# Gate and up products of an FFN by sevenfold block products: high and low part of the input joined in one matmul, low parts of stored weights by adding DMAs

## The chip, the cores and the metric

The kernel runs on one core of a Trainium2 chip. Its metric is device microseconds of one execution. A core has five engines that run side by side, each through its own list of instructions in order: TensorE (PE, with its weight loads shown apart as PEld), VectorE (DVE), ScalarE (ACT), GpSimd (POOL) and SyncE (SP). PSUM, where TensorE writes its sums, has eight banks of 512 fp32 values per partition; SBUF holds all else that is on the chip.

## The reference, cut to what matters

One layer of a decoder over 512 tokens of width 1024, all in fp32:

```python
x = x + 0.5 * RMSNorm_post(SwiGLU_1(RMSNorm_pre(x)))    # FFN 1
h = RMSNorm_pre(x)
y = mixer(h)                    # dilated attention, mLSTM, gates, output projection
x = x + RMSNorm_post(y)
x = x + 0.5 * RMSNorm_post(SwiGLU_2(RMSNorm_pre(x)))    # FFN 2

def swiglu(x, w_gate, w_up, w_down):    # 1024x2816, 1024x2816, 2816x1024
    return (silu(x @ w_gate) * (x @ w_up)) @ w_down
```

Only the gate and up products of the two FFNs, silu(x @ w_gate) * (x @ w_up), are the subject here.

## The kernel before, in words

Every large matmul is made of three: each fp32 value v is cast to a shorter type (fp32r) as its high part h, and v - h is its low part l. A product of weights and input is then h h + h l + l h, summed in PSUM. Casts run on ScalarE, the subtractions on VectorE. In the names below wh and wl are the parts of a weight, hTh and hTl those of the normalised input, which lies transposed (1024 on partitions in 8 chunks, 512 tokens along the free axis; `new_hT`, line 211, two tiles).

The hidden width 2816 is cut into 22 blocks f of 128. In each FFN f = 0 and 1 go through `by_halves` and f = 2 through `ws`, both plain. The 19 blocks f = 3 to 21 go through `seven` (lines 299 to 419), a scheme in the manner of Strassen and Winograd. It takes the two weight blocks of one f, gate g and up u, each cut into two halves of the 1024 sums (g0, g1, u0, u1, 128x512 each with four chunks of 128 side by side), and the input cut into 2x2 blocks, halves of the sums by halves of the tokens (256 tokens each). Instead of eight block products it makes seven, numbered 1 to 7, whose factors are sums of blocks:

- weights: 1 = g0, 2 = g1, 4 = u1 as stored; 7 = ab0 = g0 + u0 and 5 = ab1 = u0 + u1; 6 = cd0 = ab0 + u1 and 3 = cd1 = cd0 + g1. Signs are in the stored weights.
- input: made once per FFN by `token_parts` (line 269): parts 1, 2, 3 are blocks of hTh and hTl, parts 4 to 7 are sums, split anew in tiles of their own.

One `product` (line 336) is 12 matmuls of 256 columns: for each of the four chunks, wh times the input's high part and wh times its low part, and then wl times the high part for each chunk. A unit (one f) has thus 84 matmuls. Its results stand in two PSUM banks, one column half each: bank qa holds a (products 1 and 2: gate, first tokens; the copy q1 takes product 1 alone), bank qb holds b (6, then 7, then 4) and c (5, then 3) in its two halves. VectorE and ScalarE combine them:

- q1 = copy of a behind product 1 (ScalarE)
- uv = (b, c) + q1 behind products 6 and 5, one operation over the whole bank qb
- `inner`, behind products 7 and 3: z1 = b + uv1 and z2 = c + uv0, two operations of 256 columns
- `finish`, behind product 4, which goes on into b: z0 = b + q1, then aT = -(z0, z1) * s in one operation (aT is the FFN's hidden activation)
- silu(0): s0 = silu(a) behind product 2; silu(1): s1 = silu(z2)

The weights' path per unit: `load` issues two DMAs of 512 KB (g and u) on SP into tiles wf (three buffers, line 311). `take` casts a pair of blocks to wh on ScalarE and returns the subtraction that makes wl on VectorE; it is used for (1, 2) from g (`front`), (4) from u1, (6, 3) from cd and (7, 5) from ab. `sums` are four additions on VectorE. Tiles wh and wl have five buffers, those of (4) two; scr tiles: ab, cd, uv and s one buffer each, q1 and z two.

The order of each engine is written out by hand. `do` is an object of class `Order` (line 259): it issues each instruction behind the last one of the same engine, so VectorE, ScalarE, POOL and SP run exactly in program order, and all of these instructions carry line 265 in the trace. TensorE runs in program order too (line 340). The loop (lines 376 to 417) goes over units u, with v the next unit and w the one after. TensorE's order for one u is product 1 of u, 6, 5, product 4 of the previous unit, then 2, 7, 3 of u. Between them stand, in program order: `inner` and silu(1) of the previous unit; q1; the low part of (1, 2) of v; the loads of w; `sums` of v and the cast of cd; uv; the low part of cd; z0 and aT of the previous unit; the cast and low part of (4) of v; silu(0) of u; the cast and low part of ab of v; the cast of g of w.

A PSUM tile comes from `bank` (line 62), a pool of eight banks in rotation (line 60), which all stages of the kernel share. Behind `seven` follows the down projection, its first part also sevenfold (class `Down`, 35 steps). It is a generator: its first pieces (loads, sums, splits and `banks` for eight accumulators, lines 583 to 585) run between the last units of `seven` by `next(ahead)`. Its weights are summed by adding DMAs on POOL's queue (`add`, accum_op=ADD), its T and S tiles take the buffers of hTh and hTl (lines 587 and 588). `ffn` (line 607) puts the stages together, lines 638 to 650.

Of the kernel before, what the change touches and what calls it, by code (L numbers as in the profile page):

```python
# [10 lines left out]
F32 = mybir.dt.float32  # L11
# [28 lines left out]
def tile_hybrid_block(ctx: ExitStack, tc: tile.TileContext, a: dict):  # L40
# [153 lines left out]
    def by_halves(groups, hTh, hTl, todo):  # L194
        for hf in range(2):
            tok = slice(hf * T // 2, (hf + 1) * T // 2)
            for n, (outs, ws_) in enumerate(groups):
# [4 lines left out]
                for i, b in order:  # L202
# [5 lines left out]
                    if hf == 0 and b and (n, i) in FLUSH:  # L208
                        flush(todo)

    def new_hT(name):
        hTh = hpool.tile([P, KD, T], F32R, tag="hTh", name=f"hTh_{name}")
        hTl = hpool.tile([P, KD, T], F32R, tag="hTl", name=f"hTl_{name}")
        return hTh, hTl

# [53 lines left out]
    def token_parts(low, tmp, hTh, hTl, name):  # L269
        def quad(t, i, j):  # L270
            return t[:, 4 * i:4 * i + 4, j * H:(j + 1) * H]

        hf, xs_ = tmp[:, 0:8, :], tmp[:, 8:16, :]
        for j in (1, 0):
            for i in (1, 0):
                with tc.issue_after(opened[0]):
                    nc.vector.tensor_tensor(quad(hf, i, j), quad(hTh, i, j).bitcast(F32),
                                            quad(hTl, i, j).bitcast(F32), op=ADD)
        b11, b12, b21, b22 = (quad(hf, i, j) for i in range(2) for j in range(2))
        f = {k: xs_[:, 2 * i:2 * i + 2, :].rearrange("p a (b c) -> p (a b) c", c=H) for i, k in enumerate((5, 6, 7, 4))}  # L280
        parts = {1: (quad(hTh, 0, 0), quad(hTl, 0, 0)), 2: (quad(hTh, 1, 0), quad(hTl, 1, 0)),
                 3: (quad(hTh, 1, 1), quad(hTl, 1, 1))}

        def part(k):
            xh, xl = (low.tile([P, 4, H], F32R, name=f"x{k}{x}_{name}") for x in "hl")
            split(f[k], xh, xl)
            parts[k] = (xh, xl)
# [11 lines left out]
    def seven(do, fs, wgu, x, low, scr, aT, name, ahead):  # L299
        tt = lambda out, p, q, op: do("vector", "tensor_tensor", out, p, q, op=op)  # L300
        cast = lambda out, p: do("scalar", "copy", out, p)

        class Unit:
# [3 lines left out]
            def load(self):  # L307
                self.gu = []
                for b in range(2):
                    t = act.tile([P, 2, Q], F32, tag="wf", bufs=3, name=f"{'gu'[b]}_{self.n}")  # L310
                    nc.sync.dma_start(t, wgu[self.f, :, b * 1024:(b + 1) * 1024].rearrange("p (q c) -> p q c", c=Q))
                    self.gu.append(t)

            def take(self, keys, src, n=2):
                pool, tag, bufs = (wpool, "", 5) if n == 2 else (low, "4", 2)
# [20 lines left out]
            def product(self, out, k, first, last):  # L336
                (wh, wl), (xh, xl) = self.w[k], x[k]
                terms = [(wh, y, i) for i in range(4) for y in (xh, xl)] + [(wl, xh, i) for i in range(4)]
                for n, (wt, y, i) in enumerate(terms):
                    nc.tensor.matmul(out, lhsT=wt[:, i * P:(i + 1) * P], rhs=y[:, i, :], start=first and n == 0,  # L340
                                     stop=last and n == len(terms) - 1, skip_group_check=True)

            def open(self):
                n = self.n
                self.pa, self.pb = bank(f"qa_{n}"), bank(f"qb_{n}")
                self.q1 = scr.tile([P, H], F32, tag="q1", bufs=2, name=f"q1_{n}")
                self.uv = scr.tile([P, 2, H], F32, tag="uv", bufs=1, name=f"uv_{n}")
                self.z = scr.tile([P, 3, H], F32, tag="z", bufs=2, name=f"z_{n}")
                self.s = scr.tile([P, 2, H], F32, tag="s", bufs=1, name=f"s_{n}")
                self.a, self.b, self.c = self.pa[:, 0:H], self.pb[:, 0:H], self.pb[:, H:T]  # L350
# [15 lines left out]
        for u in us[:2]:  # L366
            u.load()
            u.front()
            if u is us[0]:
                u.low12()  # L370
                u.sums()
                u.lowcd()
                u.take((4,), u.gu[1][:, 1:2, :], 1)()
                u.take((7, 5), u.ab)()
        prev = None
        for i in range(len(fs)):
# [21 lines left out]
            if v:  # L398
# [32 lines left out]
    class Down:  # L431
# [138 lines left out]
        def run(self):  # L570
# [11 lines left out]
            self.split(s1, "x")  # L582
            ba, bd, bc, bb = (self.banks(*x) for x in (("a", (0, 1), 0), ("d", (2, 3), 1), ("c", (0, 1), 1),
                                                       ("b", (2, 3), 0)))
            self.out = {"1": bd, "2": ba, "3": bc, "4": bb, "5": bc, "6": bb, "7": bb}
            self.product(s0)
            self.T = hpool.tile([P, KD, T], F32, tag="hTh", name=f"T_{self.name}")
            self.S = hpool.tile([P, KD, T], F32, tag="hTl", name=f"S_{self.name}")
            for g in range(4):
                self.do("sync", "dma_start", self.U(g), self.B(g, BLOCK["1"]))  # L590
            yield
            self.T4 = self.xp.tile([P, self.n4, T], F32, tag="u4", bufs=1, name=f"T4_{self.name}")
            self.S4 = self.xp.tile([P, self.n4, H], F32, tag="s4", bufs=1, name=f"S4_{self.name}")
# [13 lines left out]
    def ffn(pool, todo, first_w, hT, wgu, wdq, wdh, wd, post, finish, name, begin=None, pins=(), aT=None):  # L607
# [1181 lines left out]
```

## Time and profile before

| | us |
|---|---|
| runs, three: lowest, median, highest | 1311.48, 1312.67, 1314.56 |
| profiled execution, its own time | 1310.56 |
| its span, first to last instruction | 1308.6 |
| TensorE busy | 1300.7 (99%) |
| TensorE weight loads busy | 1179.0 (90%) |
| VectorE busy | 1039.5 (79%) |
| ScalarE busy | 658.2 (50%) |
| GpSimd busy | 124.9 (10%) |
| granted TensorE clock, mean | 0.999 |
| moved by DMA | 182.72 MB, mean 140 GB/s |

The profile is that of one execution. Busy times are sums of instruction durations, and matmuls overlap, so the durations of single matmuls (0.28 us for one of 256 columns) are longer than the distance from one start to the next. In a table by line, a row gives the line, the engine, the operation, the output and inputs with their shape, the count, the busy time and the mean of one in ns, then the idle time of the engine ahead of them and what ended it. In a row of the timeline the first number is the start in us, the second the duration; a bracket gives a wait of the engine ahead of the instruction and its releaser. The names of tiles carry _a in FFN 1 and _b in FFN 2. A DMA's row gives its queue (SPq, POOLq), its size and the time from issue to landing.

### The profile page before, as it was taken

How to read it: one execution, taken by the hardware profiler on the slowest of the kernel's cores; microseconds unless marked ns; L12 is line 12 of the kernel's file. 1: busy time of each engine (PE TensorE's matmuls, PEld its weight loads, DVE VectorE, ACT ScalarE, POOL GpSimd, SP SyncE). 2: the span in 40 equal slices, each digit the busy share in tenths (PEclk: the TensorE clock that was granted, in tenths of full speed). 3: DMA queues.
4: the chain of work that ended last, by engine and by line, in shares of the span. 5: the costliest groups of instructions: out<-in, count | busy, mean ns of one | idle time of the engine just before them, and what ended most of it. 6: DMA issues, size and time to landing. Idle time of an engine off the chain costs nothing.

```text
span 1308.6 us, 20788 instructions
## 1 busy us (share of the span) xinstructions
PE 1300.7 (99%) x8173; PEld 1179.0 (90%) x8173; DVE 1039.5 (79%) x1599; ACT 658.2 (50%) x1065; POOL 124.9 (10%) x175
## 2 busy tenths in 40 slices
PE   9999999999999999999999999999999999999997
PEld 9999999888899888888888889998889999999886
DVE  7999988888895577577798687666389998897887
ACT  6444444566644546435555554434265444445563
POOL 1000000231302110011112010000010000001220
PEclk9999999999999999999999999999999999999999
DMA  5233333696458974257637532334412333325981
GB/s 195 96 113 97 112 101 111 180 245 152 152 170 223 320 91 134 68 158 183 210 90 178 169 97 65 102 108 161 168 61 81 111 101 110 112 99 155 268 174 65
DMA packets 52114, 182.72 MB, mean 140 GB/s; under 512 B 6133, under 2 KB 7181, under 8 KB 51761
## 3 DMA queue, kind: packets, MB, share of 16 engines
q1 hardware_dynamic: 32832, 116.18, 27.0%
q0 software_dynamic: 19168, 65.22, 20.9%
q8 instruction: 64, 1.05, 0.3%
q14 instruction: 34, 0.27, 0.1%
q10 hardware_dynamic: 16, 0.00, 0.0%
HBM read 171.87 MB, written 9.46 MB: 139 GB/s over the span
## 4 chain that ended last, share of the span: by engine, by line
PE 99%; DVE 1%; POOL 0%; issue 0%; ACT 0%; DVEq 0%; POOLq 0%; ACTq 0%
PE qb_a L340 10%; PE qb_b L340 10%; PE pq L191 8%; PE pm L191 7%; PE qa_b L340 4%; PE qa_a L340 4%; PE qb_gm L1209 4%; PE acc_o L245 3%; PE accb_b L539 3%; PE vo1p L940 3%; PE vo0p L940 3%; PE w12p L940 3%; PE accb_a L539 3%; PE accc_b L539 2%; PE accc_a L539 2%; PE pg_a L205 2%
## 5 line engine op out<-in xcount | busy, mean ns | idle before, releaser
L191 PE MATMUL pq<-hTh_mx,wh_qk 128*128 128x512 f32 x160 | 63.2, 395 | 0.0
L191 PE MATMUL pq<-hTl_mx,wh_qk 128*128 128x512 f32 x160 | 62.4, 390 | 0.0
L191 PE MATMUL pm<-hTh_mx,wh_mqk 128*128 128x512 f32 x128 | 50.4, 394 | 0.0
L191 PE MATMUL pm<-hTl_mx,wh_mqk 128*128 128x512 f32 x128 | 49.9, 390 | 0.0
L101 DVE TENSOR_TENSOR wl_qk<-wf_qk,wh_qk 128x1024 fp32r<-128x1024 f32 x24 | 29.3, 1221 | 17.6 <-ACT wh_qk L85 13.5
L265 ACT CAST wh_a<-cd_a 128x1024 fp32r<-128x1024 f32 x19 | 19.9, 1049 | 40.8 <-DVE cd_a L265 40.8
L265 ACT CAST wh_b<-cd_b 128x1024 fp32r<-128x1024 f32 x19 | 19.9, 1049 | 40.5 <-DVE cd_b L265 40.5
L191 PE MATMUL pq<-hTh_mx,wl_qk 128*128 128x512 f32 x160 | 39.5, 389 | 0.0
L85 ACT CAST wh_qk<-wf_qk 128x1024 fp32r<-128x1024 f32 x24 | 25.0, 1045 | 28.6 <-PE pq L191 12.1
L340 PE MATMUL qa_b<-hTh_f,wh_b 128*128 128x256 f32 x152 | 38.2, 284 | 0.0
L340 PE MATMUL qa_a<-hTh_f,wh_a 128*128 128x256 f32 x152 | 38.2, 284 | 0.0
L340 PE MATMUL qa_b<-hTl_f,wh_b 128*128 128x256 f32 x152 | 38.1, 283 | 0.0
L340 PE MATMUL qa_a<-hTl_f,wh_a 128*128 128x256 f32 x152 | 38.1, 283 | 0.0
L1117 DVE SCALAR_TENSOR_TENSOR z<-pm,cw,z 128x511 f32<-128x511 f32 (+2 forms) x48 | 35.3, 743 | 2.2 <-ACT z L1115 1.8
L191 PEld LDWEIGHTS pq<-hTh_mx,wl_qk 128*128 128x128 f32 x160 | 30.0, 188 | 6.2
L191 PEld LDWEIGHTS pq<-hTh_mx,wh_qk 128*128 128x128 f32 x160 | 30.1, 188 | 6.0
L191 PEld LDWEIGHTS pq<-hTl_mx,wh_qk 128*128 128x128 f32 x160 | 30.1, 188 | 6.0
L265 DVE TENSOR_TENSOR wl_b<-ab_b,wh_b 128x1024 fp32r<-128x1024 f32 x19 | 23.3, 1225 | 15.0 <-ACT wh_b L265 15.0
L265 DVE TENSOR_TENSOR wl_a<-ab_a,wh_a 128x1024 fp32r<-128x1024 f32 x19 | 23.3, 1225 | 14.7 <-ACT wh_a L265 14.7
L265 POOL DMA_DIRECT2D T_a<-in_wdq x12 | 10.9, 1155 | 238.3 <-DVE xl_a L265 228.9
L265 POOL DMA_DIRECT2D T_b<-in_wdq x12 | 10.6, 1127 | 236.6 <-PE acca_b L539 225.7
L101 DVE TENSOR_TENSOR wl_mqk<-wf_mqk,wh_mqk 128x1024 fp32r<-128x1024 f32 x16 | 19.5, 1220 | 16.2 <-PE pq L191 8.4
(1021 smaller groups left out, 4654.6 us busy)
## 6 DMA issues: line engine op xcount, KB each, us to landing
wf_qk<-in_wqk SPq DMA_DIRECT2D x24, 512.0 KB, 4.2
g_a<-in_wgu SPq DMA_DIRECT2D x19, 512.0 KB, 3.7
u_a<-in_wgu SPq DMA_DIRECT2D x19, 512.0 KB, 3.7
g_b<-in_wgu SPq DMA_DIRECT2D x19, 512.0 KB, 3.7
u_b<-in_wgu SPq DMA_DIRECT2D x19, 512.0 KB, 3.7
wf_mqk<-in_wmqk SPq DMA_DIRECT2D x16, 512.0 KB, 3.6
wf_vo<-in_wvo SPq DMA_DIRECT2D x16, 512.0 KB, 3.7
T_a<-in_wdq POOLq DMA_DIRECT2D x12, 512.0 KB, 10.3
```

The lines of the kernel that those rows point to most:

```text
L85: return nc.scalar.copy(wh, wf)
L101: last_low[0] = nc.vector.tensor_tensor(wl[:, :m], wf[:, :m], wh[:, :m].bitcast(F32), op=ALU.subtract).ins
L191: nc.tensor.matmul(out, lhsT=wt[:, k * P:(k + 1) * P], rhs=x[:, k, 0:T], start=n == 0, stop=n == len(terms) - 1)
L205: nc.tensor.matmul(outs[b][:, tok], lhsT=ws_[b][w][:, k * P:(k + 1) * P], rhs=x[:, k, tok], start=i + k + hf == 0, stop=hf == 1 and i == 2 ...
L245: nc.tensor.matmul(out, lhsT=x[:, tk], rhs=w[:, cs], start=first and n == 0, stop=last and n == 2, skip_group_check=True)
L265: self.last[eng] = getattr(getattr(nc, eng), fn)(*args, **kw).ins
L340: nc.tensor.matmul(out, lhsT=wt[:, i * P:(i + 1) * P], rhs=y[:, i, :], start=first and n == 0, stop=last and n == len(terms) - 1, skip_gro ...
L539: nc.tensor.matmul(o, lhsT=x[:, tk], rhs=w[:, cs], start=k in "1256" and g + m + n == 0, stop=False, skip_group_check=True)
L940: nc.tensor.matmul(out[k][i], lhsT=x[:, 2 * g + m, i * P:(i + 1) * P], rhs=y[:, m * T:(m + 1) * T], start=k in "156" and g + m + j == 0, s ...
L1117: nc.vector.scalar_tensor_tensor(z[:, s:], src[:, :T - s], cw[:, ct, 3 - s:4 - s], z[:, s:], op0=ALU.mult, op1=ALU.add)
L1209: nc.tensor.matmul(out, lhsT=wt[:, i * P:(i + 1) * P], rhs=y[:, i, :], start=first and m == 0, stop=last and m == len(terms) - 1, skip_gro ...
```

## The change

It has these parts, all in `seven` and what surrounds it.

- The input's high and low parts lie in one tile. `new_hT` allocates one tile [128, 2, 8, 512], and hTh and hTl are its two halves; parts 4 to 7 get one tile [128, 2, 4, 256] each. For products 3 to 7 the matmul with wh then takes 512 columns in one instruction, 256 of the high part and 256 of the low part; the result fills a whole bank, wh times high in its first half (`high`) and wh times low in its second (`low`). The matmul with wl goes into the first half. A product is then 4 matmuls of 512 columns and 4 of 256. Products 1 and 2 keep their 12 of 256 in a half bank.
- b and c need a whole bank each, a pair `qbc`, two such pairs in rotation, and a has a bank `qa`, two in rotation: six banks, in a pool `pairs` that is open during `seven` alone. For this the pool of eight becomes one of two (`psum2`), open throughout, and one of six that is closed ahead of `seven` and opened again behind it (`Banks`); `bank` goes through the six and then the two. `Down` takes the two banks of `psum2` ahead of the others, which it takes when the pairs are closed.
- The halves are added on VectorE: `outer` (high + q1, then low + that) in place of uv's one operation, over (b, c), 512 columns each; `inner` two operations of 512 in place of two of 256; z0 two of 256 in place of one.
- The low parts of the weights that are used as stored, (1, 2) and (4), are no longer subtracted on VectorE. ScalarE writes -wh into wl (`mul` by -1, behind the cast), and an adding DMA on POOL's queue adds the stored weights to it from HBM (`stored`), 512 KB for (1, 2) and 256 KB for (4). These two VectorE operations of 1024 and 512 columns go.
- `Down`'s T and S become one tile, in the buffer of the joined hT.

The diff, cut to its core:

```diff
     def bank(name):
-        return psum.tile([P, 512], F32, tag="pp", name=name)
+        pool = banks.pool if banks.n % 8 < 6 else psum2
+        banks.n += 1
+        return pool.tile([P, 512], F32, tag="pp", name=name)
...
     def new_hT(name):
-        hTh = hpool.tile([P, KD, T], F32R, tag="hTh", name=f"hTh_{name}")
-        hTl = hpool.tile([P, KD, T], F32R, tag="hTl", name=f"hTl_{name}")
-        return hTh, hTl
+        whole_of.append(hpool.tile([P, 2, KD, T], F32R, tag="hT", name=f"hT_{name}"))
+        return whole_of[-1][:, 0], whole_of[-1][:, 1]
...
-            def take(self, keys, src, n=2):
+            def take(self, keys, src, n=2, stored=None):
...
                 cast(wh, src)
-                return lambda: tt(wl, src, wh.bitcast(F32), SUB)
+                if stored is None:
+                    return lambda: tt(wl, src, wh.bitcast(F32), SUB)
+                do("scalar", "mul", wl, wh.bitcast(F32), -1.0)
+                do("gpsimd", "dma_start", wl, stored, accum_op=ADD)
...
             def front(self):
-                self.low12 = self.take((1, 2), self.gu[0])
+                self.take((1, 2), self.gu[0], 2, self.stored(0))
...
             def product(self, out, k, first, last):
-                (wh, wl), (xh, xl) = self.w[k], x[k]
-                terms = [(wh, y, i) for i in range(4) for y in (xh, xl)] + [(wl, xh, i) for i in range(4)]
-                for n, (wt, y, i) in enumerate(terms):
-                    nc.tensor.matmul(out, lhsT=wt[:, i * P:(i + 1) * P], rhs=y[:, i, :], start=first and n == 0,
-                                     stop=last and n == len(terms) - 1, skip_group_check=True)
+                (wh, wl), y = self.w[k], x[k]
+                cols = lambda i: slice(i * P, (i + 1) * P)
+                if k > 2:
+                    terms = [(out, wh[:, cols(i)], y[:, :, i, :]) for i in range(4)]
+                else:
+                    terms = [(out, wh[:, cols(i)], y[:, j, i, :]) for i in range(4) for j in range(2)]
+                terms += [(out[:, 0:H], wl[:, cols(i)], y[:, 0, i, :]) for i in range(4)]
+                for n, (o, w, v) in enumerate(terms):
+                    nc.tensor.matmul(o, lhsT=w, rhs=v, start=first and n == 0, stop=last and n == len(terms) - 1,
+                                     skip_group_check=True)
...
             def open(self):
                 n = self.n
-                self.pa, self.pb = bank(f"qa_{n}"), bank(f"qb_{n}")
+                self.a = pairs.tile([P, 512], F32, tag="qa", bufs=2, name=f"qa_{n}")[:, 0:H]
+                self.bc = pairs.tile([P, 2, 512], F32, tag="qbc", bufs=2, name=f"qbc_{n}")
+                self.b, self.c = self.bc[:, 0], self.bc[:, 1]
+                self.high, self.low = self.bc[:, :, 0:H], self.bc[:, :, H:T]
...
+            def outer(self):
+                z = self.z[:, 1:3, :]
+                tt(z, self.high, self.q1[:, None, :].broadcast_to([P, 2, H]), ADD)
+                tt(self.uv[:, ::-1, :], self.low, z, ADD)
 
             def inner(self):
-                tt(self.z[:, 1, :], self.b, self.uv[:, 1, :], ADD)
-                tt(self.z[:, 2, :], self.c, self.uv[:, 0, :], ADD)
+                z = self.z[:, 1:3, :]
+                tt(z, self.high, self.uv, ADD)
+                tt(z, self.low, z, ADD)
...
             def finish(self):
                 self.product(self.b, 4, False, False)
-                tt(self.z[:, 0, :], self.b, self.q1, ADD)
+                z = self.z[:, 0, :]
+                tt(z, self.b[:, 0:H], self.q1, ADD)
+                tt(z, self.b[:, H:T], z, ADD)
...
-            if v:
-                v.low12()
             u.product(u.b, 6, True, False)
...
-            u.product(u.c, 5, False, False)
-            tt(u.uv, u.pb.rearrange("p (a b) -> p a b", b=H), u.q1[:, None, :].broadcast_to([P, 2, H]), ADD)
+            u.product(u.c, 5, True, False)
+            u.outer()
...
             if v:
-                low4 = v.take((4,), v.gu[1][:, 1:2, :], 1)
-                low4()
+                v.take((4,), v.gu[1][:, 1:2, :], 1, v.stored(1)[:, 1:2, :])
...
         ahead = d.run()
-        last = seven(do, range(PLAIN, NF), wgu, x, low, scr, aT, name, ahead)
+        banks.ctx.close()
+        banks.n = 6
+        pctx = ExitStack()
+        pairs = pctx.enter_context(tc.tile_pool(name=f"pairs_{name}", bufs=2, space=bass.MemoryType.PSUM,
+                                                reuse_waits="tile"))
+        last = seven(do, range(PLAIN, NF), wgu, x, low, scr, pairs, aT, name, ahead)
         dn = ExitStack()
         next(ahead)
         last()
+        pctx.close()
+        banks.open(f"psum6_{name}")
```

More of the change, by code (lines that the diff above doesn't have):

```diff
@@ L59, in tile_hybrid_block, with open @@
     small = ctx.enter_context(tc.tile_pool(name="small", bufs=4, side="right"))
-    psum = ctx.enter_context(tc.tile_pool(name="psum", bufs=8, space=bass.MemoryType.PSUM))
+    psum2 = ctx.enter_context(tc.tile_pool(name="psum2", bufs=2, space=bass.MemoryType.PSUM))
+    class Banks:
+        ctx, pool, n = None, None, 0
+        def open(self, name, n=0):
+            self.ctx, self.n = ExitStack(), n
+            self.pool = self.ctx.enter_context(tc.tile_pool(name=name, bufs=6, space=bass.MemoryType.PSUM))
+    banks = Banks()
+    banks.open("psum6")
+    ctx.callback(lambda: banks.ctx.close())
     def bank(name):
-        return psum.tile([P, 512], F32, tag="pp", name=name)
+        pool = banks.pool if banks.n % 8 < 6 else psum2
+        banks.n += 1
+        return pool.tile([P, 512], F32, tag="pp", name=name)
     def pair(name):
@@ L209, in by_halves @@
                         flush(todo)
+    whole_of = []
     def new_hT(name):
-        hTh = hpool.tile([P, KD, T], F32R, tag="hTh", name=f"hTh_{name}")
-        hTl = hpool.tile([P, KD, T], F32R, tag="hTl", name=f"hTl_{name}")
-        return hTh, hTl
+        whole_of.append(hpool.tile([P, 2, KD, T], F32R, tag="hT", name=f"hT_{name}"))
+        return whole_of[-1][:, 0], whole_of[-1][:, 1]
     def down(n, chunk_src, get_x, post, finish, todo, name, accs=None, first=0):
@@ L280, in token_parts @@
         f = {k: xs_[:, 2 * i:2 * i + 2, :].rearrange("p a (b c) -> p (a b) c", c=H) for i, k in enumerate((5, 6, 7, 4))}
-        parts = {1: (quad(hTh, 0, 0), quad(hTl, 0, 0)), 2: (quad(hTh, 1, 0), quad(hTl, 1, 0)),
-                 3: (quad(hTh, 1, 1), quad(hTl, 1, 1))}
+        parts = {k: whole_of[-1][:, :, 4 * i:4 * i + 4, j * H:(j + 1) * H]
+                 for k, (i, j) in {1: (0, 0), 2: (1, 0), 3: (1, 1)}.items()}
         def part(k):
-            xh, xl = (low.tile([P, 4, H], F32R, name=f"x{k}{x}_{name}") for x in "hl")
-            split(f[k], xh, xl)
-            parts[k] = (xh, xl)
+            x = low.tile([P, 2, 4, H], F32R, name=f"x{k}_{name}")
+            split(f[k], x[:, 0], x[:, 1])
+            parts[k] = x
         nc.vector.tensor_tensor(f[5], b11, b12, op=SUB)
@@ L297, in token_parts, with seven @@
         return parts
-    def seven(do, fs, wgu, x, low, scr, aT, name, ahead):
+    def seven(do, fs, wgu, x, low, scr, pairs, aT, name, ahead):
         tt = lambda out, p, q, op: do("vector", "tensor_tensor", out, p, q, op=op)
@@ L310, in load, with stored @@
                     t = act.tile([P, 2, Q], F32, tag="wf", bufs=3, name=f"{'gu'[b]}_{self.n}")
-                    nc.sync.dma_start(t, wgu[self.f, :, b * 1024:(b + 1) * 1024].rearrange("p (q c) -> p q c", c=Q))
+                    nc.sync.dma_start(t, self.stored(b))
                     self.gu.append(t)
-            def take(self, keys, src, n=2):
+            def stored(self, b):
+                return wgu[self.f, :, b * 1024:(b + 1) * 1024].rearrange("p (q c) -> p q c", c=Q)
+            def take(self, keys, src, n=2, stored=None):
                 pool, tag, bufs = (wpool, "", 5) if n == 2 else (low, "4", 2)
@@ L369, in seven @@
             if u is us[0]:
-                u.low12()
                 u.sums()
                 u.lowcd()
-                u.take((4,), u.gu[1][:, 1:2, :], 1)()
+                u.take((4,), u.gu[1][:, 1:2, :], 1, u.stored(1)[:, 1:2, :])
                 u.take((7, 5), u.ab)()
@@ L582, in run @@
             self.split(s1, "x")
-            ba, bd, bc, bb = (self.banks(*x) for x in (("a", (0, 1), 0), ("d", (2, 3), 1), ("c", (0, 1), 1),
-                                                       ("b", (2, 3), 0)))
-            self.out = {"1": bd, "2": ba, "3": bc, "4": bb, "5": bc, "6": bb, "7": bb}
+            self.out = {"2": self.banks("a", (0, 1), 0)}
             self.product(s0)
-            self.T = hpool.tile([P, KD, T], F32, tag="hTh", name=f"T_{self.name}")
-            self.S = hpool.tile([P, KD, T], F32, tag="hTl", name=f"S_{self.name}")
+            TS = hpool.tile([P, 2, KD, T], F32, tag="hT", name=f"TS_{self.name}")
+            self.T, self.S = TS[:, 0], TS[:, 1]
             for g in range(4):
@@ L591, in run @@
             yield
+            bd, bc, bb = (self.banks(*x) for x in (("d", (2, 3), 1), ("c", (0, 1), 1), ("b", (2, 3), 0)))
+            self.out.update({"1": bd, "3": bc, "4": bb, "5": bc, "6": bb, "7": bb})
             self.T4 = self.xp.tile([P, self.n4, T], F32, tag="u4", bufs=1, name=f"T4_{self.name}")
```

1 line of the change is left out of this document (removed).

## The prediction

> **What bounds the kernel now.** I read the busy table of the page first, then its chain of waits, then the table of stages.
>
> ```profile
> span 1308.6 us, 20788 instructions
> PE 1300.7 (99%) x8173; PEld 1179.0 (90%) x8173; DVE 1039.5 (79%) x1599; ACT 658.2 (50%) x1065; POOL 124.9 (10%) x175
> ...
> PE 99%; DVE 1%; POOL 0%; issue 0%; ACT 0%; DVEq 0%; POOLq 0%; ACTq 0%
> PE qb_a L340 10%; PE qb_b L340 10%; PE pq L191 8%; PE pm L191 7%; PE qa_b L340 4%; PE qa_a L340 4%; PE qb_gm L1209 4%; PE acc_o L245 3%; PE accb_b L539 3%; PE vo1p L940 3%; PE vo0p L940 3%; PE w12p L940 3%; PE accb_a L539 3%; PE accc_b L539 2%; PE accc_a L539 2%; PE pg_a L205 2%
> ```
>
> The chain is TensorE from end to end, and line 340, the sevenfold products, is 28% of it. Only this stage is touched in earnest, so I went on with it: it runs twice, from 46.6 to 236 us and from 1003.9 to 1193.
>
> ```profile
> core 0: us, PE busy (x) PEld busy (x) DVE busy (x) ACT busy (x) POOL busy (x), PEclk, DMA share, GB/s
> 66.70:157.00 90.30, 90.30 (x755) 90.30 (x754) 81.45 (x120) 41.62 (x63) 0.00 (x0) 1.00 0.33 108
> 1023.00:1184.00 161.00, 161.00 (x1344) 161.00 (x1343) 144.71 (x209) 74.09 (x112) 0.00 (x0) 1.00 0.32 106
> ```
>
> TensorE never pauses, but VectorE is busy 90% of the time. A share cannot say whether that leaves room, so I laid out one unit (one value of f), first VectorE, then the two ScalarE instructions that VectorE waits for, then three starts on TensorE (product 1 of this unit, its product 7, product 1 of the next).
>
> ```profile
> 146.50 0.76 DVE L265 TENSOR_TENSOR z_a<-qb_a,uv_a 128x256 f32<-128x256 f32 x2
> 147.18 1.21 DVE L265 TENSOR_TENSOR wl_a<-g_a,wh_a 128x1024 fp32r<-128x1024 f32 x1
> 148.31 0.68 DVE L265 TENSOR_TENSOR ab_a<-g_a,u_a 128x512 f32<-128x512 f32 x1
> 149.03 0.69 DVE L265 TENSOR_TENSOR cd_a<-ab_a,u_a 128x512 f32<-128x512 f32 x1
> 149.75 0.69 DVE L265 TENSOR_TENSOR cd_a<-cd_a,g_a 128x512 f32<-128x512 f32 x1
> 150.36 0.68 DVE L265 TENSOR_TENSOR ab_a<-u_a 128x512 f32<-128x512 f32 x1
> 150.96 0.68 DVE L265 TENSOR_TENSOR uv_a<-qb_a,q_a 128x512 f32<-128x512 f32 x1
> 151.56 1.22 DVE L265 TENSOR_TENSOR wl_a<-cd_a,wh_a 128x1024 fp32r<-128x1024 f32 x1
> 152.70 0.42 DVE L265 TENSOR_TENSOR z_a<-qb_a,q_a 128x256 f32<-128x256 f32 x1
> 153.15 0.69 DVE L265 SCALAR_TENSOR_TENSOR aT_a<-z_a,s_a 128x512 f32<-128x512 f32 x1
> 153.76 0.68 DVE L265 TENSOR_TENSOR wl_a<-u_a,wh_a 128x512 fp32r<-128x512 f32 x1
> 155.31 1.23 DVE L265 TENSOR_TENSOR wl_a<-ab_a,wh_a 128x1024 fp32r<-128x1024 f32 x1 [0.87 <-ACT wh_a L265]
> 156.59 0.42 DVE L265 TENSOR_TENSOR z_a<-qb_a,uv_a 128x256 f32<-128x256 f32 x1
> ```
> ```profile
> 153.96 0.39 ACT L265 ACTIVATE s_a<-qa_a 128x256 f32<-128x256 f32 x1 [1.55 <-DVE aT_a L265]
> 154.24 1.04 ACT L265 CAST wh_a<-ab_a 128x1024 fp32r<-128x1024 f32 x1
> 155.18 1.05 ACT L265 CAST wh_a<-g_a 128x1024 fp32r<-128x1024 f32 x1
> ```
> ```profile
> 146.31 0.28 PE L340 MATMUL qa_a<-hTh_f,wh_a 128*128 128x256 f32 x1
> ...
> 153.50 0.28 PE L340 MATMUL qb_a<-x7h_a,wh_a 128*128 128x256 f32 x1
> ...
> 156.38 0.28 PE L340 MATMUL qa_a<-hTh_f,wh_a 128*128 128x256 f32 x1
> ```
>
> There is a second ring beside TensorE's. The order is fixed per engine, and VectorE's instructions run one behind the other from `inner` (146.50) to the aT product of `finish` (153.15). `silu(0)` must wait for that product, since the tile s has one buffer (153.15 + 0.69 = 153.84, start 153.96). The cast of ab stands behind it on ScalarE, its low part (155.31) waits for the cast, and the next `inner` comes behind that low part. A split of 1024 leads to the next start in 1.14 (151.56 to 152.70), so `inner` could start at 156.45 and starts at 156.59: the ring is 9.95 long where TensorE's unit is 156.38 - 146.31 = 10.07. TensorE bounds the stage by 0.12 us per unit, no more.
>
> **The change part by part.** Joined matmuls. Products 3 to 7 of a unit lose 4 instructions each, 20 in all: two of 256 columns become one of 512. A 256-wide one takes 10.07 / 84 = 120 ns from start to start. A 512-wide one stands in the plain products ahead of the stage, 24 of them between these two starts:
>
> ```profile
> 35.66 0.40 PE L191 MATMUL pg_a<-hTh_f,wh_agu 128*128 128x512 f32 x1
> ...
> 41.13 0.39 PE L191 MATMUL pg_a<-hTh_f,wh_agu 128*128 128x512 f32 x1
> ```
>
> That is 228 ns, so a joined pair saves 240 - 228 = 12 ns, a unit 0.24 us, and TensorE's unit becomes 9.83; 38 units give 9.1 us if nothing else binds. The joined operand is read in two runs of 256; no row has that. Bounds are 228 (as one run) and 240 (no gain); I take 228, the row of the same size. The Trainium skill, "TensorE: Matmul & The Clock Gate", section "Back-to-back issue gap", gives N / 2.4 + 2.5 ns, so 109 and 216 ns; by that a pair would save 2.6 ns and the whole 2.0 us, but the trace's 120 and 228 are what counts here.
>
> VectorE, per unit, by starts in the rows above. `inner`: two operations of 256 (146.50 to 147.18, 0.68) become two of 512, the second on the first's result. Such a pair is 0.72 apart (148.31 to 149.03), and the next follows 0.61 later (149.75 to 150.36): 1.33, so +0.65. The low part of (1, 2) at 147.18 goes: -1.13. The uv sum (0.60) becomes the pair `outer`, 0.72 + 0.61: +0.73. The z sum of `finish` (0.45) becomes two: +0.45. The low part of (4) at 153.76 goes too, but it lay inside the wait for ScalarE: 0. Together +0.70, though VectorE's busy time falls. The ring becomes 9.95 + 0.70 = 10.65, longer than TensorE's old unit and far longer than its new one. So VectorE and ScalarE set the stage, and TensorE waits some 0.8 us per unit, at product 7, which must not write bank b before `outer` has read it. The new operations read two banks in two runs, which no row has. Below: if dependent pairs close up as independent ones do (0.60 and 0.34 for 0.72 and 0.45), 10.30. Above: if each 512 from two banks costs like two of 256 (0.76 for 0.68), 10.97. I take 10.65, as the uv row reads PSUM at the price of SBUF.
>
> ScalarE gets two multiplications per unit. A cast of 1024 is 1.05 above; a multiplication of 512 is 0.63:
>
> ```profile
> L87 ACT ACTIVATE wh_ad<-wf_ad 128x512 fp32r<-128x512 f32 x4 | 2.5, 626 | 0.0
> ```
>
> So 1.05 to 1.25, and 0.63. ScalarE was busy 41.62 of 90.30, 4.6 per unit; with 1.9 more it fits into 10.65. The one of (4) stands ahead of `silu(0)`, but starts when product 4 of the unit before is through, some 2 us ahead; the one of (1, 2) stands behind the cast of ab, off the ring, and ends 0.7 us before the next `silu(1)` could start. Cost 0; without that cover it lengthens the ring by its excess.
>
> Adding DMAs: 512 KB and 256 KB per unit from POOL, 29 MB more over both stages, on a queue that issued nothing there. Behind a waiting add stands only the next add.
>
> ```profile
> u_a<-in_wdq POOLq DMA_DIRECT2D x3, 512.0 KB, 5.5
> ```
> ```profile
> T_a<-in_wdq POOLq DMA_DIRECT2D x12, 512.0 KB, 10.3
> ```
> ```profile
> 283.00:300.00 17.00, 17.00 (x77) 14.08 (x76) 16.93 (x25) 8.83 (x13) 8.76 (x10) 1.00 0.90 172
> ```
>
> The first row is three adds 2.3 to 3.5 us apart, the second adds issued close upon one another. Here they come some 5 us apart, so I take 5.5. With `inner` at 0 the cast of ab starts at 8.4, that of (1, 2) at 9.4, its multiplication at 10.3; the add is issued at 11.4 and lands at 16.9. Product 7 starts at 5.4 when `outer` is through, products 7 and 3 take 2.8, so product 1 of the unit after next starts at 5.4 + 2.8 + 10.65 = 18.9 and needs the low part 0.96 later, at 19.8. There are 2.9 us to spare, and about 1.9 more before a late product 1 makes `outer` late. What hides the add is thus a whole unit; it costs from a landing of about 10.3 us on. The part for (4) is issued earlier and used five products later. Loads on SP come no later: the stored tiles are let go earlier.
>
> The ends of a stage. In the first unit nothing hides `outer`; product 7 starts right behind uv:
>
> ```profile
> 52.83 0.69 DVE L265 TENSOR_TENSOR uv_a<-qb_a,q_a 128x512 f32<-128x512 f32 x1 [1.00 <-ACT wh_a L265]
> ```
> ```profile
> 53.57 0.39 PE L340 MATMUL qb_a<-x7h_a,wh_a 128*128 128x256 f32 x1
> ```
>
> So +0.73 there, -0.19 by its 16 pairs. In the last unit there are no sums and splits, and TensorE gains its 0.24. TensorE also has a lead to use up first: uv ended at 151.64 and product 7 started at 153.50; in the new order `outer` ends at 146.50 + 1.33 + 2.65 + 0.72 + 0.69 = 151.89 and product 7 could start at 153.36, so 1.47 us of lag never reach the end.
>
> PSUM pools of 6 and 2 in place of 8, the joined tile hT for two, banks taken later in Down: in the stages around, a bank still comes round after eight; 0, at most one VectorE operation (0.7) per change of pool.
>
> The sum per FFN: 17 units with a neighbour on both sides, 17 x (10.65 - 10.07) = +9.9; -1.47 lead; -0.24 last; +0.54 first: +8.7. Twice: +17.4. The profiled execution took 1310.56 us (span 1308.6 and 2 around it), which gives 1328.0; it lies 2.1 under the median of the runs, 1312.67, which gives 1330.1. I take 1329.
>
> **The rivals.** TensorE keeps the pace (faster). VectorE's busy time per unit falls by about 0.2 us, to under 9 of 9.83, so if the wait of `silu(0)` were no part of a ring (s free in time) the stage would follow TensorE: 2 x (18 x -0.24 + 0.54) = -7.6, so 1305. For it: the page's share, 79% against 99%. Against: 153.15 to 155.31 in the rows above, where ScalarE waits 1.55 and then VectorE 0.87, in every unit. It decides if the ring is under 9.83. By the skill's gaps this rival would end at 1312, no change.
>
> No change: the ring comes out near 10.1, if the new pairs close up and the strided reads are cheaper than any row: 1311 to 1315.
>
> The adds come late (slower still). If the two loads of 512 KB per unit and the adds crowd one another as in the second row, to 12 us, then 1.7 us beyond 10.3 are spread over two units: 17 x 0.85 = 14.5 per FFN, so 1358. For: loads and adds overlap. Against: the stage moves 108 GB/s at a DMA share of 0.33. The Trainium skill, "SBUF — State Buffer", warns in its box on DVE blocking DMA that a GpSimd-issued DMA starves for descriptors while VectorE holds their shared port; the row of 283 to 300 us has VectorE busy 16.93 of 17.00 and adds landing in 5.5, so it doesn't bind there.
>
> That joining does nothing (240 ns per joined matmul) would change little: the ring is longer than either; 1329 to 1331.
>
> **How the numbers follow.** The ring 0.69, its own range 1317 (10.30) to 1340 (10.97); late adds 0.07; TensorE's pace 0.17; no change 0.07. The range 1304 to 1342 takes in the faster case's 1305 and leaves out the late adds and whatever of the faster case lies lower. The time comes from the likeliest. What a measurement here can tell is about 0.2%, 2.6 us: faster 0.17, same 0.07, slower 0.76.
>
> **What would show it.** In a middle unit: VectorE's `inner` to `inner` at 10.65, with no wait on TensorE and one of some 1.55 before the low part of ab; TensorE pausing about 0.8 us before product 7; joined matmuls 228 apart; adds landing in 5 to 7 us and no wait of qa for wl. I am wrong if `inner` to `inner` is 9.8 with VectorE waiting for product 3, if TensorE waits at product 1's low part, or if other stages move by more than 1 us.

## The result, and the profile after

The changed kernel took 1335.42 us (median of 5 runs, 1334.69 to 1337.8), the kernel before 1312.17 (5 runs, 1311.46 to 1314.56): the ratio is 1.0178, with a 95% interval of 1.0163 to 1.0193. The forecast was 1329 and slower, with a range of 1304 to 1342. So direction and range held, and the size was short: the forecast sum for the profiled execution was +17.4 us, and the spans differ by 1332.8 - 1308.6 = 24.2. The range says little by itself, since it also held the faster case and the case of no change.

The page of the changed kernel: span, busy times, and the chain of waits by engine.

```profile
span 1332.8 us, 19598 instructions
PE 1301.6 (98%) x7413; PEld 1138.5 (85%) x7413; DVE 1036.3 (78%) x1599; ACT 717.6 (54%) x1141; POOL 190.7 (14%) x251
...
PE 64%; issue 20%; DVE 9%; POOL 3%; ACT 2%; DMA 1%; POOLq 0%; DVEq 0%; ACTq 0%
```

The chain, TensorE from end to end before, now leaves TensorE for a third of the span. VectorE's share of busy time went down by a point, as its 1036.3 us against 1039.5 says, and yet the stage follows it. In a middle stretch of the stage TensorE is no longer always busy (columns as in the table of stretches ahead: from:to, length, busy times, clock, DMA share, GB/s):

```profile
85.00:225.00 140.00, 133.50 (x848) 119.32 (x846) 118.49 (x172) 82.15 (x119) 23.01 (x27) 1.00 0.74 174
```

One unit of the changed kernel. First VectorE from `inner` to `inner`, then the two ScalarE instructions of the ring, then TensorE over one unit, up to where it pauses and two products on (rows with wl are left out but for the two of bank qa), then the waits of these 140 us summed by releaser:

```profile
144.22 0.68 DVE L279 TENSOR_TENSOR z_a<-qbc_a,uv_a 128x512 f32<-128x512 f32 x1
144.94 0.69 DVE L279 TENSOR_TENSOR z_a<-qbc_a,z_a 128x512 f32<-128x512 f32 x1
145.55 0.68 DVE L279 TENSOR_TENSOR ab_a<-g_a,u_a 128x512 f32<-128x512 f32 x1
...
148.20 0.68 DVE L279 TENSOR_TENSOR z_a<-qbc_a,q_a 128x512 f32<-128x512 f32 x1
...
149.53 1.22 DVE L279 TENSOR_TENSOR wl_a<-cd_a,wh_a 128x1024 fp32r<-128x1024 f32 x1
150.66 0.42 DVE L279 TENSOR_TENSOR z_a<-qbc_a,q_a 128x256 f32<-128x256 f32 x1
151.11 0.43 DVE L279 TENSOR_TENSOR z_a<-qbc_a,z_a 128x256 f32<-128x256 f32 x1
151.57 0.69 DVE L279 SCALAR_TENSOR_TENSOR aT_a<-z_a,s_a 128x512 f32<-128x512 f32 x1
153.71 1.22 DVE L279 TENSOR_TENSOR wl_a<-ab_a,wh_a 128x1024 fp32r<-128x1024 f32 x1 [1.45 <-ACT wh_a L279]
154.85 0.68 DVE L279 TENSOR_TENSOR z_a<-qbc_a,uv_a 128x512 f32<-128x512 f32 x1
```
```profile
152.36 0.39 ACT L279 ACTIVATE s_a<-qa_a 128x256 f32<-128x256 f32 x1 [2.35 <-DVE aT_a L279]
152.64 1.04 ACT L279 CAST wh_a<-ab_a 128x1024 fp32r<-128x1024 f32 x1
```
```profile
143.69 1.09 PE L365 MATMUL qbc_a<-x_a,wh_a 128*128 128x512 f32 x4
...
145.09 1.09 PE L365 MATMUL qbc_a<-x_a,wh_a 128*128 128x512 f32 x4
146.01 0.40 PE L365 MATMUL qa_a<-hT_f,wh_a 128*128 128x256 f32 x2
...
146.72 0.88 PE L365 MATMUL qa_a<-hT_f,wh_a 128*128 128x256 f32 x6
147.44 1.09 PE L365 MATMUL qbc_a<-x_a,wh_a 128*128 128x512 f32 x4
...
148.84 1.12 PE L365 MATMUL qa_a<-hT_f,wh_a 128*128 128x256 f32 x8
149.79 0.64 PE L365 MATMUL qa_a<-hT_f,wl_a 128*128 128x256 f32 x4
151.08 0.74 PE L365 MATMUL qa_a<-hT_f,wl_a 128*128 128x256 f32 x4 [0.65 <-DMA wl_a<-in_wgu]
151.66 1.08 PE L365 MATMUL qbc_a<-x_a,wh_a 128*128 128x512 f32 x4
...
153.05 1.09 PE L365 MATMUL qbc_a<-hT_f,wh_a 128*128 128x512 f32 x4
```
```profile
ACT s_a L279 <- DVE aT_a L279: 30.3, 13, 2.4
DVE wl_a L279 <- ACT wh_a L279: 18.8, 13, 1.4
...
PE qa_a L365 <- DMA wl_a<-in_wgu: 6.3, 13, 0.7
```

`inner` to `inner` is 154.85 - 144.22 = 10.63 us, with the wait for ScalarE in it, 1.45 in each unit, and no wait of VectorE for TensorE. That is the ring as forecast (10.65). TensorE's pause stands in another place than forecast: at four matmuls of bank qa with wl, released by the adding DMA, and not at product 7. Which product that is follows from the order of the rows. A product on bank qa is eight matmuls with wh and then four with wl. Between products 6 (143.69), 5 (145.09) and 4 of the unit before (147.44) on one side and products 7 (151.66) and 3 (153.05) on the other, two such products stand: one begins with the two and six matmuls at 146.01 and 146.72, the other with the eight at 148.84. The four with wl at 149.79 close the second, product 2. The four that wait, at 151.08, close the first, and that is product 1 of the NEXT unit, which in program order comes only behind products 7 and 3. The add fits this: products 1 and 2 of a unit share one tile wl, and the four of product 2 at 149.79 found theirs landed.

Only VectorE, ScalarE, POOL and SP are held in order by `do`; TensorE's instructions are put in order by the planner that builds the program. In the middle units of the kernel before it left them in program order; in the changed one it put product 1 of the next unit ahead of product 7. The trace before shows this freedom in the first unit: there product 1 of the second unit starts at 52.56, ahead of product 7 at 53.57.

Where the 24 us lie, from the starts of these instructions in the two traces (before and after, FFN 1 and one row of FFN 2; a bracket gives the wait of the row's engine):

```profile
46.57 0.28 PE L340 MATMUL qa_a<-hTh_f,wh_a 128*128 128x256 f32 x1
...
56.74 0.42 DVE L265 TENSOR_TENSOR z_a<-qb_a,uv_a 128x256 f32<-128x256 f32 x1 [0.36 <-PE qb_a L340]
...
237.22 0.76 DVE L265 TENSOR_TENSOR z_a<-qb_a,uv_a 128x256 f32<-128x256 f32 x2 [0.26 <-PE qb_a L340]
...
241.20 1.09 PE L539 MATMUL acca_a<-wh_a,xh_a 128*128 128x512 f32 x4
```
```profile
48.60 1.19 PE L365 MATMUL qa_a<-hT_f,wh_a 128*128 128x256 f32 x8 [1.91 <-DVE aT_a L648]
...
59.20 0.69 DVE L279 TENSOR_TENSOR z_a<-qbc_a,uv_a 128x512 f32<-128x512 f32 x1 [0.87 <-PE qbc_a L365]
...
249.97 0.68 DVE L279 TENSOR_TENSOR z_a<-qbc_a,uv_a 128x512 f32<-128x512 f32 x1
...
252.93 0.62 PE L570 MATMUL acca_a<-wh_a,xh_a 128*128 128x512 f32 x2
...
1017.83 0.95 PE L365 MATMUL qa_b<-hT_f,wh_b 128*128 128x256 f32 x6 [1.97 <-DVE aT_b L648]
```

| stretch | FFN 1, us | FFN 2, us |
|---|---|---|
| ahead of the first product (from the run's start, from the stage before) | +2.03 | +2.23 |
| first product to first `inner` | +0.43 | +0.41 |
| first to last `inner`, 18 units | 190.77 - 180.48 = +10.29 | +10.79 |
| last `inner` to the down projection's next matmul | -1.02 | -1.01 |

Together 24.15, and the last matmul of the program, too, comes 24.15 us later than before. The 0.5 more in FFN 2 is one unit of 11.08 us, in which TensorE waits 1.20 us for an add and VectorE then 0.37 for product 3. So a wait of 0.65 for an add hides behind the ring, and one of 1.20 no longer does: the adds come just in time.

### The profile page after: what moved, and what is told of

Same layout as the page of the kernel before. It is cut to its first block, busy times and chain, and to the rows that moved or that the text cites. A ratio compares the mean times of both kernels' runs of the same rounds, so it can differ in the third digit from the quotient of the medians.

```text
span 1332.8 us, 19598 instructions
## 1 busy us (share of the span) xinstructions
PE 1301.6 (98%) x7413; PEld 1138.5 (85%) x7413; DVE 1036.3 (78%) x1599; ACT 717.6 (54%) x1141; POOL 190.7 (14%) x251
## 4 chain that ended last, share of the span: by engine, by line
PE 64%; issue 20%; DVE 9%; POOL 3%; ACT 2%; DMA 1%; POOLq 0%; DVEq 0%; ACTq 0%
PE pq L204 8%; PE pm L204 7%; PE qb_gm L1247 4%; PE acc_o L259 3%; PE accb_b L570 3%; PE w12p L978 3%; PE vo1p L978 3%; PE vo0p L978 3%; PE accb_a L570 3%; PE accc_b L570 2%; PE accc_a L570 2%; POOL wl_a L279 2%; PE pq L218 2%; PE qa_gm L1247 2%; DVE wl_b L279 1%
## 5 line engine op out<-in xcount | busy, mean ns | idle before, releaser
L365 PE MATMUL qbc_a<-x_a,wh_a 128*128 128x512 f32 x304 | 83.2, 394 | 0.5 <-DVE z_a L279 0.5
L365 PE MATMUL qbc_b<-x_b,wh_b 128*128 128x512 f32 x304 | 83.3, 395 | 0.4 <-DVE z_b L279 0.4
L204 PE MATMUL pq<-hT_mx,wh_qk 128*128 128x512 f32 x320 | 76.9, 392 | 0.0
L204 PEld LDWEIGHTS pq<-hT_mx,wh_qk 128*128 128x128 f32 x320 | 59.4, 188 | 12.0
L204 PE MATMUL pm<-hT_mx,wh_mqk 128*128 128x512 f32 x256 | 61.3, 392 | 0.0
L365 PEld LDWEIGHTS qbc_a<-x_a,wh_a 128*128 128x128 f32 x304 | 52.1, 189 | 7.9 <-DVE z_a L279 0.9
L365 PEld LDWEIGHTS qbc_b<-x_b,wh_b 128*128 128x128 f32 x304 | 52.1, 189 | 7.9 <-DVE z_b L279 0.8
L204 PEld LDWEIGHTS pm<-hT_mx,wh_mqk 128*128 128x128 f32 x256 | 47.4, 188 | 9.5
L365 PE MATMUL qbc_a<-x_a,wl_a 128*128 128x256 f32 x304 | 48.3, 281 | 0.0
L365 PE MATMUL qbc_b<-x_b,wl_b 128*128 128x256 f32 x304 | 48.3, 281 | 0.0
```

What stands on the lines that cost most here:

```text
L204: nc.tensor.matmul(out, lhsT=wt[:, k * P:(k + 1) * P], rhs=x[:, k, 0:T], start=n == 0, stop=n == len(terms) - 1)
L365: nc.tensor.matmul(o, lhsT=w, rhs=v, start=first and n == 0, stop=last and n == len(terms) - 1, skip_group_check=True)
```

## The experiments

Each kernel is one edit of the changed kernel or of the kernel before. The kernel before was timed beside each group: 1312.33 us for the first four, 1311.0 for the next four, 1311.52 for the last. Ratios are to it; the changed kernel's own is 1.0178.

**TensorE in program order.** Does the wait for the adding DMA set the pace, as TensorE's row suggests?

```diff
-                    nc.tensor.matmul(o, lhsT=w, rhs=v, ...)
+                    do("tensor", "matmul", o, lhsT=w, rhs=v, ...)
```

> The changed kernel with TensorE's sevenfold matmuls held in program order (in the changed kernel the planner put product 1 of the next unit ahead of product 7 of this one, and TensorE there waits some 0.65 to 0.8 us per unit for the low part that the adding DMA brings). Theory of the ring (silu(0) waits for aT, the cast of ab stands behind it, the low part of ab behind that, inner behind that): the ring does not contain TensorE's order, so inner to inner stays at 10.62 us, TensorE's 0.8 us of waiting per unit moves to product 7 and is released by VectorE, and the time stays at 1333 to 1337. Rival, the late adds set the pace: with product 1 back in its place the adds have some 6 us more, the wait goes, the unit falls to TensorE's 9.83 and the time to about 1307.

Measured: 1338.58 us, ratio 1.0200 (1.0186 to 1.0214), 1.6 us above the upper end of the theory's range, and not faster at all. The waits of the same 140 us:

```profile
ACT s_a L279 <- DVE aT_a L279: 31.3, 13, 2.4
...
DVE wl_a L279 <- ACT wh_a L279: 18.8, 13, 1.4
...
PE qbc_a L279 <- DVE uv_a L279: 6.1, 13, 0.5
```

The wait for the DMA is gone, the same 6 us stand at product 7 and are released by `outer`, and the ring's two waits are what they were; `inner` to `inner` is 10.63 in every middle unit. Late adds are no cause of the unit's 10.63 us. This trace is 3.8 us longer than the changed kernel's (1336.6 against 1332.8). In the first unit in program order product 2 waits 0.46 us for q1 and product 7 1.58 us for `outer`, a time that product 1 of the next unit fills in the changed kernel; with it the second `inner` of FFN 1 comes 1.1 us later. In FFN 2 the same waits recur, and behind the wait ahead of the stage the granted clock is 0.66 from 1019.8 to 1024.8 us, so that products 1 and 2 there take 1.2 us more. Another 0.8 lies between the two stages, and its cause stays open.

**The cast of ab ahead of silu(0).** The ring cut at one place, by order alone.

```diff
+                low75 = v.take((7, 5), v.ab) if v else None
                 u.silu(0)
             if v:
-                v.take((7, 5), v.ab)()
+                low75()
```

> The changed kernel with one thing moved on ScalarE: the cast of ab is issued ahead of silu(0) and not behind it, so that the low part of ab on VectorE no longer hangs on aT of the unit before. Theory of the ring: VectorE's pitches without the wait sum to 9.1 us per unit, below TensorE's 9.83, so the unit becomes 9.83; per FFN -3.9 us between the first and the last inner against the kernel before, +0.4 at the first unit, -0.7 at the last, +1.9 for the wait ahead of the stage, so about -2.2, and the time is 1307 to 1310. Rival, VectorE's own work (operations on two banks) is the bound and not the wait: the unit stays above 10.3, 1325 or more. Rival, late adds: TensorE waits for wl as before, above 1325.

Measured: 1308.62 us, ratio 0.9975 (0.9965 to 0.9985): faster than the changed kernel by 2%, and than the kernel before by 0.25%; the interval ends below 1. VectorE now goes on from aT to the low part of ab without a pause and waits for TensorE ahead of `inner`, and TensorE is always busy:

```profile
144.32 0.69 DVE L279 SCALAR_TENSOR_TENSOR aT_a<-z_a,s_a 128x512 f32<-128x512 f32 x1
144.93 1.22 DVE L279 TENSOR_TENSOR wl_a<-ab_a,wh_a 128x1024 fp32r<-128x1024 f32 x1
146.51 0.69 DVE L279 TENSOR_TENSOR z_a<-qbc_a,uv_a 128x512 f32<-128x512 f32 x1 [0.37 <-PE qbc_a L365]
```
```profile
85.00:225.00 140.00, 140.00 (x907) 127.42 (x906) 128.53 (x184) 90.22 (x127) 24.50 (x28) 1.00 0.81 189
```

The unit is 9.89 us (146.51 to 156.40), TensorE's own pace. The first two units take only some 9.1 us each from `inner` to `inner`: that is VectorE's own work without a wait, as forecast, until it has caught up with TensorE. The planner also put TensorE's middle units back into program order in this kernel, but the first experiment has shown that this order alone leaves the ring where it was.

**The banks of f = 2.** Can the 1.9 us ahead of the stage be had back?

```diff
+            banks.n = 6
             pg = pair(f"pg_{name}{f}")
```

> The changed kernel with the two banks of the plain products f = 2 taken from the pool of two that stays open, so that the first sevenfold unit finds its six banks long read. TensorE waited 1.9 and 2.0 us there, once per FFN, for the aT product of f = 2. Theory, that wait is lost time: -3.9 us, 1331 to 1332. Rival, the ring swallows it (the first unit's product 7 waits for outer anyway and inner comes no earlier): 1334 to 1336.

Measured: 1334.19 us, ratio 1.0167 (1.0154 to 1.0181), so 1.2 us below the changed kernel where 3.9 were looked for; the two intervals overlap, and the time lies in the rival's range. The bank wait is gone, and TensorE pauses a few products later:

```profile
52.28 1.12 PE L365 MATMUL qa_a<-hT_f,wh_a 128*128 128x256 f32 x8
55.47 0.74 PE L365 MATMUL qa_a<-hT_f,wl_a 128*128 128x256 f32 x4 [2.08 <-DMA wl_a<-in_wgu]
```

The first `inner` stands at 59.26 where it stood at 59.20. The rival's outcome was right, but not its reason: it was not `outer` that swallowed the gain (it ends at 53.96 there), but the add for the second unit's (1, 2), needed early because product 1 stands early.

**Joined matmuls without the adds.** All low parts subtracted on VectorE again.

```diff
-                self.take((1, 2), self.gu[0], 2, self.stored(0))
+                self.low12 = self.take((1, 2), self.gu[0])
...
-                v.take((4,), v.gu[1][:, 1:2, :], 1, v.stored(1)[:, 1:2, :])
+                v.take((4,), v.gu[1][:, 1:2, :], 1)()
```

with low12() called where the kernel before calls it.

> The changed kernel with the low parts of (1, 2) and (4) made by subtraction on VectorE as before, without the two multiplications on ScalarE and without adding DMAs. Theory of the ring: the low part of (1, 2) comes back into it, 1.13 us; that of (4) fits into the wait for ScalarE. Inner to inner 11.75, per FFN 18 x 1.13 = +20, so 1374 to 1378. Rival, the adding DMAs are what costs: the unit falls to 9.9 to 10.1, about 1310.

Measured: 1376.97 us, ratio 1.0493 (1.0479 to 1.0508); `inner` to `inner` 11.78. The ring grows by the one split that is in it, and the adds are what keeps the changed kernel from being 3% slower still.

**Cast first, and the banks of f = 2.** Both edits above.

> The kernel of the cast ahead of silu(0), with the banks of f = 2 from the small pool as well. Without the bank wait alone the time hardly fell, and the trace showed why: in the first unit product 1 of the second stands ahead of product 7, and TensorE then waited 2.1 us for the low part of the second unit's (1, 2), whose add is issued some 48 us into the run and lands at 55.4. Theory, the one wait takes the place of the other here too: no gain on the cast ahead of silu(0), 1307 to 1309.5. Rival, with TensorE as the bound every us at the start counts: 1304 to 1306.

Measured: 1307.29 us, ratio 0.9965 (0.9955 to 0.9976), 1.3 us better than the cast alone by the medians; the two intervals overlap, so no gain is shown. TensorE's waits in the whole run name the add once per FFN, where the bank wait was:

```profile
PE qa_a L365 <- DMA wl_a<-in_wgu: 2.8, 1, 2.8
PE qa_b L365 <- DMA wl_b<-in_wgu: 1.2, 1, 1.2
```

**And the second unit's add issued early.** Cast, multiplication and add of (1, 2) of the second unit ahead of the sums and casts of the first.

```diff
         for u in us[:2]:
             u.load()
             u.front()
-            if u is us[0]:
-                u.sums()
...
+        u = us[0]
+        u.sums()
```

> The same with one more move ahead of the stage: the cast, the multiplication and the add for (1, 2) of the second unit are issued ahead of the sums and casts of the first, some 8 us earlier, where ScalarE is idle for 3.6 us. Theory, both waits of the first unit are gone and TensorE, which is the bound now, gains 1.9 to 2.0 us per FFN: 1303.5 to 1305.5. Rival, a third wait (product 7 on outer, 1.6 us when TensorE runs in program order) takes their place: 1307 or more.

Measured: 1303.34 us, ratio 0.9942 (0.9929 to 0.9955). No wait for a bank or an add is left among TensorE's, product 1's low part runs straight behind its high part, and the first `inner` comes at 57.19, 2.0 us earlier than in the changed kernel. The time is just below the range of the theory:

```profile
52.35 1.12 PE L365 MATMUL qa_a<-hT_f,wh_a 128*128 128x256 f32 x8
53.31 0.64 PE L365 MATMUL qa_a<-hT_f,wl_a 128*128 128x256 f32 x4
```

The bank wait thus had the add's wait behind it: by the ratios (0.9975, 0.9965, 0.9942) its removal alone is worth 1.3 us at most (not clear of noise), that of both 4.3 of the 7.7 us by which this version beats the kernel before. The early add alone was not run.

**The adds alone**, in the kernel before: `take` as in the change, matmuls and banks as before.

> The kernel before with only the low parts of (1, 2) and (4) by multiplication and adding DMA; the matmuls stay 12 of 256, the banks as before. Theory of the ring: VectorE's ring falls from 9.95 to 8.8, TensorE's unit of 10.08 was the bound already and stays, no wait of TensorE for wl: 1311 to 1314. Rival, the 29 MB of adds cost of themselves (TensorE waits at products 1 or 4, loads come later, or the stages around slow down): above 1318.

Measured: 1311.38 us, ratio 1.0004 (0.9995 to 1.0013). VectorE's busy time falls from 1039.5 to 977.0 us, and nothing comes of it. Nor do the adds cost anything that shows, though 212.63 MB are moved in place of 182.72; the interval ends at 0.13%.

**Cast first, without the adds.** Joined matmuls, the cast ahead of silu(0), all low parts on VectorE.

> The joined matmuls with the cast of ab ahead of silu(0), but with all low parts by subtraction on VectorE (no multiplication, no adds). Theory: VectorE's operations without a wait sum to 9.09 + 1.13 + 0.61 = 10.83 us per unit, above TensorE's 9.89, so VectorE is the bound: per FFN 18 x 10.83 - 180.8 = +14.1 between the first and last inner, +1.6 around, 1342 to 1346. Rival, the adds were of no use and the cast's place is all: 1308 to 1310.

Measured: 1348.09 us, ratio 1.0276 (1.026 to 1.0291). The unit is 10.83 as worked out: VectorE's own work bounds it, so the adds are needed for the joining to pay. The 2 to 6 us more than expected lie elsewhere, at least in part in the clock: in this trace the granted clock is 0.83 in the stretches 45 to 55, 435 to 445 and 1025 to 1035 us, where the changed kernel's trace shows 1.00; by estimate each costs up to 1.7 us (10 x 0.17). In the second of them TensorE also waits 2.5 us at w12p in the mixer, which no edit touches. What sets the lower clock and this wait off stays open.

**The cast first in the kernel before.**

> The kernel before with only the cast of ab issued ahead of silu(0). Theory: TensorE's 10.08 per unit is the bound there and VectorE's 9.95 hides behind it, so shortening the ring gives nothing, 1311 to 1313, and the gain of the joined kernel with the same move is the joining's. Rival, the move itself is what gains, in any kernel: 1306 to 1309.

Measured: 1311.08 us, ratio 0.9996 (0.9987 to 1.0005). The move gains nothing where TensorE's unit of 10.08 is the bound. The gain of 0.25% with joined matmuls is the joining's, once the ring is out of its way.

## Why the prediction was right, and where it was not

Of the three signs that the forecast named for being wrong, two came: TensorE waits at product 1's low part, and the stretch ahead of each stage grew by more than 1 us. The third, `inner` to `inner` at 9.8, did not, and it was the only one that tests the ring.

**What bounds the kernel: right.** Before, TensorE bounds the unit and a ring through silu(0) stands just behind it: adding work to VectorE turns the ring into the bound (10.63 and 11.78), and shortening it in the kernel before gives nothing.

**The ring's terms: right.** `inner` was put at 1.33 and is 145.55 - 144.22 = 1.33; `outer` at 1.33 and is 149.53 - 148.20 = 1.33; z0 at 0.90 and is 151.57 - 150.66 = 0.91; the low part of (4) at nothing, since it lay inside the wait, and the wait is still 1.45. 10.65 was forecast, 10.63 measured. The lower bound (pairs that close up) and the upper one (two banks dearer than SBUF) did not come: an operation of 512 columns over two banks in two runs takes 0.68 to 0.69 us, as one from SBUF does.

**The joined matmul: right in kind, mis-sized.** 228 ns were taken. With TensorE as the bound (cast ahead of silu(0)), the rows of products 1, then 6 and the next start give it:

```profile
146.31 1.12 PE L365 MATMUL qa_a<-hT_f,wh_a 128*128 128x256 f32 x8
...
147.75 1.09 PE L365 MATMUL qbc_a<-x_a,wh_a 128*128 128x512 f32 x4
148.68 0.63 PE L365 MATMUL qbc_a<-x_a,wl_a 128*128 128x256 f32 x4
149.15 1.09 PE L365 MATMUL qbc_a<-x_a,wh_a 128*128 128x512 f32 x4
```

(148.68 - 147.75) / 4 = 232 ns, so a pair saves 8 ns and not 12; TensorE's unit is 5 x 1.40 + 2 x 1.44 = 9.88, not 9.83. With the ring at 10.63 this changes nothing in the time of the changed kernel. The Trainium skill, "TensorE: Matmul & The Clock Gate", section "Back-to-back issue gap", gives its gap of N / 2.4 + 2.5 ns for an isolated matmul; it leaves 2.5 ns per pair (the forecast has 2.6) and fits less well here: 120 and 232 ns were measured where it has 109 and 216, and the saving is three times its own.

**ScalarE and the adds: right on the path, wrong in one step.** The multiplications cost nothing (1.06 and 0.63 us, beside waits of 1.43 and 2.35). The add for (1, 2) was put at 11.4 us behind `inner` and is issued at 156.01 - 144.22 = 11.79; it lands 5.6 later, where 5.5 was taken:

```profile
wl_a<-in_wgu POOLq DMA_DIRECT2D x19, 512.0 KB, 5.6
```

The step that failed is the time at which it is needed. It was counted to product 1 in TensorE's program order, 19.8 us behind `inner`, and nothing but the planner's choice holds that order. In the planner's order TensorE is there at 161.20, 17.0 us behind `inner`, and waits 0.42 until the add has landed. So the forecast's sign, a wait of qa for wl as proof against the ring, was a bad one: the wait came, and the ring was the bound all the same. Only the pinned order could tell the two apart. The warning of the Trainium skill, "SBUF — State Buffer", box on DVE blocking DMA, is for VectorE operations in a 2-port mode. No run here shows the mode of these operations; a busy VectorE alone did not starve the adds: it was busy 118.49 of 140.00 us, and they landed in 5.6.

**The lead of 1.47 us: wrong.** TensorE's lag behind `uv` was taken off the sum, but the end of a stage is set by `inner`, and there the kernel before had no lag to spend. On the contrary, its first seven intervals in FFN 1 were 9.95 (VectorE catching up) and only the later ones 10.08; the 18 together took 180.48, a mean of 10.03. So the ring costs 17 x 10.63 + 10.1 - 180.5 = +10.3, where the forecast had 9.9 - 1.47 = 8.4.

**The pools at "0, at most 0.7": wrong.** TensorE waited 1.91 and 1.97 us for the aT product of f = 2, since the pool of the sevenfold stage takes the six banks in a body, the ones just written among them, and not in rotation; with the banks of f = 2 taken from the other pool this wait is gone. The part that said "a bank still comes round after eight" holds within a pool and not where one pool is closed and another opened. What was missed a second time is that the add stands right behind this wait, so that it cannot be had back alone.

**The ends of a stage: by another course.** +0.54 was forecast for the first unit and +0.43 measured, but "nothing hides `outer`" is a misreading: in both traces product 1 of the second unit stands there. With TensorE held in program order the stretch is 60.01 - 48.69 = 11.32 where the kernel before has 10.17, so +1.15. The last unit gave -1.02 and -1.01, not -0.24. In the kernel before twelve matmuls of the down projection (237.02 to 239.77) stand between the last unit's products 3 and 4; in the changed one they fill TensorE's pauses earlier, and product 4 has only to wait for `inner`:

```profile
251.44 1.19 PE L365 MATMUL qbc_a<-x_a,wh_a 128*128 128x512 f32 x4 [0.48 <-DVE z_a L279]
```

**The rivals.** "TensorE keeps the pace" did not come, but its condition, s free in time, was the right one to name: with the cast out from behind silu(0) the unit is 9.89. "Late adds" as the pace of the unit is excluded by the pinned order; what late adds did cost is 0.45 us in one unit of FFN 2. "No change" needed a ring of 10.1.

Of the 24.15 us in the traces, 21.1 are the ring's (10.29 and 10.79 between the first and last `inner`, with the one late add), 3.9 the bank waits, 0.4 lie around these, and the ends give back 1.2; in the forecast these were 16.9 with the lead, 0, 0 and +0.6.

## What to carry to other kernels

Before an edit gives work to an engine with idle time, lay out the ring that this engine closes with its neighbours: a wait that comes once per unit is part of the period, and the share of busy time does not show it. Such a ring can often be cut by order alone; here moving one cast ahead of one activation turned +1.8% into -0.25%. When a wait is seen on the engine that one takes for the bound, pin or move that instruction before it is called the cause; and when removing a wait gives nothing, look a few instructions on for the next one, and take both away.

## What was not expected of the hardware

The loads on SP's queue grew slower with the adds: 512 KB landed in 3.7 us before, and in 5.1 to 5.5 with 768 KB of adds per unit on POOL's queue, while the DMA share of the stage went from 0.32 to 0.71. The adds alone, in the kernel before, do the same (5.3 to 5.5). It cost nothing here: among the waits of the stage's middle, 85 to 225 us, none is for a load.

```profile
g_a<-in_wgu SPq DMA_DIRECT2D x19, 512.0 KB, 5.5
u_a<-in_wgu SPq DMA_DIRECT2D x19, 512.0 KB, 5.1
```
